# First norm factors loaded on GpSimd's queue, the LayerNorm's mean product half a block later, and the last norm's first third in a bank of its own

## The chip, the cores and the metric

One NeuronCore of a Trainium2 chip runs the whole program. The metric is the device time of one execution in microseconds (us), the median of three runs; lower is better.

## What is computed

One step of a hybrid decoder layer (depth 1) over 288 tokens: 256 new ones of a prompt and 8 x 4 of running samples. The model width is 2048, everything is fp32.

```python
h = rmsnorm(x, norm1_g)
a, gate, z = split(h @ w_in + b_in)                # 1024, 1024, 1024 columns
u = a * sigmoid(gate)
c = silu(layernorm(depthwise_causal_conv(u_ext, conv_w, conv_b), ln_g, ln_b))
d = multiscale_pool(z_ext)                         # windows 2, 4, 8, 16
p = (d @ pool_w per group) * pool_scale
x = x + concat[c, p] @ w_out
x = x + square(relu(rmsnorm(x, norm2_g) @ w_ff1)) @ w_ff2      # 8192 wide
y = rmsnorm(x, norm_f)
```

`rmsnorm` divides each token by the root of its mean square and multiplies by a gain per channel (the norm factors); `layernorm` needs the mean over 1024 channels first and then the mean of the squared differences. The last values of `u` and `z` go out as new states.

## The kernel before

**Layout.** Channels lie on the 128 partitions and the 288 tokens along the row, so x is the tile `xT` with 16 rows of 288 per partition. A product is one TensorE matmul of a 128x128 weight block with a 128x288 piece of activations.

**Two parts per number.** Every weight and every activation is split into `hi` (rounded to fp32r) and `lo` (the rest), and each pair of blocks takes three matmuls, hi.hi, lo.hi and hi.lo. A weight block of 512 KB comes in by DMA on SyncE's queue (`wr`), ScalarE rounds it to `whi` (L273), and VectorE or GpSimd subtracts to get `wlo` (L277, L281). There are five `whi` and five `wlo` buffers, so ScalarE's next rounding waits until TensorE has finished with the weights of five splits earlier. One such half block feeds 24 matmuls.

**Order.** The code runs through a scheduler that orders each engine's instructions by its own clock model; `tc.issue_after` puts an instruction behind a named other one, so a change at one place also moves rows elsewhere. `gemm` (L309) lists its matmuls; its `between={k: f}` calls `f` ahead of the matmuls of row block k, so that a small foreign product (a sum over channels) is put in there, and `classes` picks, place by place, the next matmul of a given parity of k and part (`TURN` is such a list, 48 long).

**The start.** SyncE's queue first loads the first norm's 16 columns of factors (`vec[:, 0:NG]`, 8 KB, L198), then in turns two rows of x (`xT`, L191) and two half blocks of weights (`wr`, L187); ScalarE's queue loads the first half block itself. Meanwhile 12 fp32 matmuls of ones keep TensorE busy (`warm`, L214; each shows as two records). `first_split` (L360) rounds the weights (ScalarE L365 and L372), makes the first activations `hx` from x and the factors (VectorE L368 for row 0, ScalarE L370 for the others), and subtracts for the low parts (VectorE L374, L377).

**The LayerNorm.** While TensorE multiplies the pooled half with `w_out` in eight blocks g = 0 to 7 (48 matmuls each), VectorE ends the convolution (L478), adds up `sum_c` over channel groups (L605), and a product with ones makes the mean over channels (tile `pmean`, in `ln_mean`, L601). It stands at the very front of block 4. `ln_sums` (L608) then subtracts the mean (VectorE L611), squares (ScalarE L613), adds the squares (VectorE L617, L618), splits the sum (L251, L252) and ends with two products (tile `norm`) at the front of block 6.

**The end.** After the last block the square sums of 288 tokens go through TensorE (L756), ScalarE and VectorE (L761 to L764) to 3 x 96 factors, which three small fp32 products spread over the partitions into `rows_f` (the tile `ends`, L767) and three more into `again`. VectorE multiplies rows 0 to 11 of `xT` by `rows_f` in pieces of 1, 1, 2, 2, 3 and 3 rows (L775); ScalarE copies `again` to `rf` for GpSimd, which takes rows 12 to 15. Each piece is written out at once, on SyncE's and ScalarE's queues in turns (L776). `idle` is a PSUM tile whose first 128 columns take three matmuls that only keep TensorE busy.

## Time and profile before

| what | value |
|---|---|
| median of 3 runs | 1078.71 us (1078.56 to 1078.87) |
| the profiled execution | 1078.44 us, of which the profile's span is 1076.7 |
| TensorE busy, matmul records | 1066.2 us (99%), 8176 |
| VectorE, ScalarE, GpSimd busy | 628.2, 482.2 and 180.0 us |
| first real matmul starts | 6.40 us into the span |
| last factors' spreading starts | 1066.00 us |
| mean granted TensorE clock | 0.997 |

Times in the profile count from the span's start. A row of the timeline has start, duration, engine and line, operation, the tiles written and read, the count of merged instructions, and in square brackets how long the engine had been idle and who ended that. PE is TensorE, DVE VectorE, ACT ScalarE, POOL GpSimd, SP SyncE; a q behind the name is the engine's queue or sequencer. Ends of matmuls are modelled, so starts are the better mark.

### The profile page before, as it was taken

How to read it: one execution, taken by the hardware profiler on the slowest of the kernel's cores; microseconds unless marked ns; L12 is line 12 of the kernel's file. 1: busy time of each engine (PE TensorE's matmuls, PEld its weight loads, DVE VectorE, ACT ScalarE, POOL GpSimd, SP SyncE). 2: the span in 40 equal slices, each digit the busy share in tenths (PEclk: the TensorE clock that was granted, in tenths of full speed). 3: DMA queues.
4: the chain of work that ended last, by engine and by line, in shares of the span. 5: the costliest groups of instructions: out<-in, count | busy, mean ns of one | idle time of the engine just before them, and what ended most of it. 6: DMA issues, size and time to landing. Idle time of an engine off the chain costs nothing.

```text
span 1076.7 us, 19546 instructions
## 1 busy us (share of the span) xinstructions
PE 1066.2 (99%) x8176; PEld 1065.5 (99%) x8176; DVE 628.2 (58%) x799; ACT 482.2 (45%) x598; POOL 180.0 (17%) x192
## 2 busy tenths in 40 slices
PE   9999999999999999999999999999999999999996
PEld 9999999999999999999999999999999999999996
DVE  8899998878554544445554444455444445554553
ACT  8655654755544433334443333444433334444441
POOL 0989889423000000000000000000000000000001
PEclk9999999999999999999999999999999999999998
DMA  9897777555455555555545555555555555455522
GB/s 333 292 248 217 223 183 244 178 174 170 164 174 165 171 172 164 174 164 169 175 165 170 170 166 175 167 166 176 162 172 171 165 174 169 164 176 162 172 80 89
DMA packets 58873, 192.81 MB, mean 179 GB/s; under 512 B 6304, under 2 KB 11296, under 8 KB 58784
## 3 DMA queue, kind: packets, MB, share of 16 engines
q1 hardware_dynamic: 56336, 184.35, 52.6%
q0 software_dynamic: 1584, 5.77, 2.9%
q8 instruction: 64, 1.05, 0.4%
q10 hardware_dynamic: 864, 1.44, 0.4%
q14 instruction: 25, 0.20, 0.1%
HBM read 187.25 MB, written 4.28 MB: 178 GB/s over the span
## 4 chain that ended last, share of the span: by engine, by line
PE 79%; issue 20%; POOL 0%; DVE 0%; POOLq 0%
PE ac L304 78%; PE pp L304 1%; PE warm L214 1%; POOL xT L775 0%; POOLq L825 0%; DVE xT L748 0%; PE norm L304 0%; PE pmean L304 0%; PE mean L304 0%; DVE ones L204 0%; DVE cst L232 0%; POOLq L775 0%; DVE cst L231 0%
## 5 line engine op out<-in xcount | busy, mean ns | idle before, releaser
L273 ACT CAST whi<-wr 128x1024 fp32r<-128x1024 f32 (+1 forms) x332 | 346.4, 1043 | 541.5 <-PE ac L304 524.6
L277 DVE TENSOR_TENSOR wlo<-wr,whi 128x1024 fp32r<-128x1024 f32 x282 | 346.2, 1228 | 349.3 <-ACT whi L273 349.2
L304 PE MATMUL ac<-ax,whi 128*128 128x288 f32 x2048 | 351.1, 292 | 0.0
L304 PE MATMUL ac<-fx,whi 128*128 128x288 f32 x2048 | 350.2, 292 | 0.0
L304 PEld LDWEIGHTS ac<-ax,whi 128*128 128x128 f32 x2048 | 296.0, 187 | 0.0
L304 PEld LDWEIGHTS ac<-fx,whi 128*128 128x128 f32 x2048 | 295.7, 187 | 0.0
L304 PE MATMUL ac<-ax,wlo 128*128 128x288 f32 x1024 | 217.4, 292 | 0.0
L304 PE MATMUL ac<-fx,wlo 128*128 128x288 f32 x1024 | 216.4, 292 | 0.0
L304 PEld LDWEIGHTS ac<-ax,wlo 128*128 128x128 f32 x1024 | 162.6, 187 | 0.0
L304 PEld LDWEIGHTS ac<-fx,wlo 128*128 128x128 f32 x1024 | 162.3, 187 | 0.0
L775 POOL TENSOR_TENSOR xT<-xT,rf 128x288 f32<-128x288 f32 x4 | 3.1, 791 | 786.6 <-ACT rf L779 786.6
L304 PE MATMUL ac<-hx,whi 128*128 128x288 f32 x768 | 130.1, 293 | 0.0
L304 PEld LDWEIGHTS ac<-hx,whi 128*128 128x128 f32 x768 | 110.6, 187 | 0.2
L281 POOL TENSOR_TENSOR wlo<-wr,whi 128x512 fp32r<-128x512 f32 x78 | 104.3, 1394 | 19.9 <-ACT whi L273 17.4
L478 DVE SCALAR_TENSOR_TENSOR pc<-u_all,vec,pc 128x256 f32<-128x256 f32 x232 | 99.3, 481 | 5.0 <-ACT pc L475 3.6
L304 PE MATMUL ac<-hx,wlo 128*128 128x288 f32 x384 | 79.5, 292 | 0.0
L304 PEld LDWEIGHTS ac<-hx,wlo 128*128 128x128 f32 x384 | 60.3, 187 | 0.1
L304 PE MATMUL ac<-dx,whi 128*128 128x288 f32 x256 | 45.9, 294 | 0.0
L304 PE MATMUL ac<-mx,whi 128*128 128x288 f32 x256 | 44.5, 292 | 0.0
L711 DVE SCALAR_TENSOR_TENSOR t<-ac,r 128x576 f32<-128x576 f32 x32 | 24.2, 757 | 25.4 <-PE ac L304 25.3
L304 PEld LDWEIGHTS ac<-dx,whi 128*128 128x128 f32 x256 | 38.1, 188 | 0.1
L304 PEld LDWEIGHTS ac<-mx,whi 128*128 128x128 f32 x256 | 37.4, 187 | 0.0
(142 smaller groups left out, 541.8 us busy)
## 6 DMA issues: line engine op xcount, KB each, us to landing
wr<-in_w SPq DMA_DIRECT2D x335, 512.0 KB, 3.6
wlo<-in_w POOLq DMA_DIRECT2D x11, 512.0 KB, 9.3
xT<-in_xT SPq DMA_DIRECT2D x8, 288.0 KB, 7.3
wr<-in_w SPq DMA_DIRECT2D x5, 256.0 KB, 4.0
out_u_out<-u_all SPq DMA_DIRECT2D x1, 1208.0 KB, 8.9
u_all<-in_hist_c SPq DMA_DIRECT2D x8, 136.0 KB, 5.5
out_z_out<-z_all SPq DMA_DIRECT2D x1, 668.0 KB, 8.6
z_all<-in_hist_p SPq DMA_DIRECT2D x4, 152.0 KB, 6.9
```

The lines of the kernel that those rows point to most:

```text
L214: nc.tensor.matmul(warm[:, 0, 0:P], ones, ones, start=True, stop=True)
L273: nc.scalar.copy(hi, raw)
L277: nc.vector.tensor_tensor(lo, raw, f32(hi), op=ALU.subtract)
L281: nc.gpsimd.tensor_tensor(lo[:, j : j + 2, :], raw[:, j : j + 2, :], f32(hi[:, j : j + 2, :]), op=ALU.subtract)
L304: last = nc.tensor.matmul(*args, **kw)
L478: nc.vector.scalar_tensor_tensor(out=dst, in0=up[:, w : w + SEQ], scalar=cwv[:, w : w + 1], in1=pc, op0=ALU.mult, op1=ALU.add)
L711: nc.vector.scalar_tensor_tensor(out=t, in0=bk[:, :, :T], scalar=0.0, in1=both(rows2[0]), op0=ALU.max, op1=ALU.mult)
L775: eng.tensor_tensor(xk, xk, r[:, None, :].to_broadcast([P, n, T]), op=ALU.mult)
```

## The change

Four edits. The load of the first norm factors moves from SyncE's queue to GpSimd's, so that x is the first load on SyncE's queue; in `first_split` the row-0 activations come ahead of the weight subtraction on VectorE, and the second rounding of a pair behind the ScalarE activations. `ln_mean` is called ahead of row block 4 of w_out block 4 instead of row block 0, and `TURN` goes from block 4 to block 5. At the end the first 96 of the 288 last factors are spread into a part of `idle` (`ahead_f`, another PSUM bank than `ends`); VectorE multiplies the first 96 tokens of rows 0 to 3 by them first, then tokens 96 to 287 of the pieces as before, with the first 96 tokens of rows 4 to 11 in between.

```diff
--- before.py
+++ after.py
@@ -195,7 +195,7 @@
             first_weights(k, nc.scalar, slice(0, 1))
             first_weights(k, nc.sync, slice(1, 2))
 
-    nc.sync.dma_start(vec[:, 0:NG], io["vec"][:, 0:NG])
+    nc.gpsimd.dma_start(vec[:, 0:NG], io["vec"][:, 0:NG])
     for k in range(0, 12, 2):
         first_load(k)
 
@@ -365,13 +365,15 @@
         nc.scalar.copy(hi[:, blocks[0]], raw[:, blocks[0]])
         for k in range(k0, k0 + 2):
             if k == 0:
-                nc.vector.tensor_scalar(hx[k][0], xT[:, k, :], v("norm1_g", k), None, op0=ALU.mult)
+                opening = [nc.vector.tensor_scalar(hx[k][0], xT[:, k, :], v("norm1_g", k), None, op0=ALU.mult)]
             else:
                 scaled.append(nc.scalar.activation(hx[k][0], xT[:, k, :], AF.Copy, scale=v("norm1_g", k)))
         for b in blocks[1:]:
-            nc.scalar.copy(hi[:, b], raw[:, b])
+            with tc.issue_after(scaled[-1].ins):
+                nc.scalar.copy(hi[:, b], raw[:, b])
         for b in blocks:
-            nc.vector.tensor_tensor(lo[:, b], raw[:, b], f32(hi[:, b]), op=ALU.subtract)
+            with tc.issue_after(opening[0].ins) if k0 == 0 else nullcontext():
+                nc.vector.tensor_tensor(lo[:, b], raw[:, b], f32(hi[:, b]), op=ALU.subtract)
         for k in (k0 + 1, k0):
             hh, hl = hx[k]
             nc.vector.scalar_tensor_tensor(out=hl, in0=xT[:, k, :], scalar=v("norm1_g", k), in1=f32(hh), op0=ALU.mult, op1=ALU.subtract)
@@ -619,13 +621,13 @@
         norm["rows"], last = row_of_sums(ssc[:, 0, :], "norm2", None, float(DC) / D, AF.Silu, parts=True)
         return last
 
-    BETWEEN = {4: {0: ln_mean}, 6: {0: ln_sums}}
+    BETWEEN = {4: {4: ln_mean}, 6: {0: ln_sums}}
     behind = nullcontext()
     for g in range(8):
         bk = bks[g] if g < 2 else bank2()
         if g > 1:
             with behind:
-                last = gemm(each(bk), proj, between=BETWEEN.get(g, {}), classes=TURN if g in (4, 6) else "")
+                last = gemm(each(bk), proj, between=BETWEEN.get(g, {}), classes=TURN if g in (5, 6) else "")
         behind = tc.issue_after(last) if g > 3 else nullcontext()
         x2 = xT[:, 2 * g : 2 * g + 2, :]
         nc.vector.tensor_tensor(x2, x2, bk[:, :, :T], op=ALU.add)
@@ -751,6 +753,7 @@
     ends, again = ms("ends"), cvp.tile([P, 512], F32, name="again", tag="cv")[:, :T]
     sums_f, rows_f = ends[:TB, 0, 0:3], ends[:, 1, :T]
     idle = cvp.tile([P, 512], F32, name="idle", tag="cv")
+    ahead_f = idle[:, P : P + TB]
     for n, (part, busy) in enumerate(((ssf, 0), (qf, 3))):
         for j in range(3):
             last = nc.tensor.matmul(sums_f[:, j : j + 1], part[:, j * TB : (j + 1) * TB], mean_d[:, 0:1], start=n + j == 0, stop=n == 1 and j == 2)
@@ -764,18 +767,28 @@
     nc.vector.scalar_tensor_tensor(out=s_f, in0=root, scalar=1.5, in1=first, op0=ALU.add, op1=ALU.mult)
     for spread_f in (rows_f, again):
         for j in range(3):
-            nc.tensor.matmul(spread_f[:, j * TB : (j + 1) * TB], s_f[:, j : j + 1].to_broadcast([TB, P]), ident, start=j == 0, stop=j == 2)
+            out = ahead_f if j == 0 and spread_f is rows_f else spread_f[:, j * TB : (j + 1) * TB]
+            nc.tensor.matmul(out, s_f[:, j : j + 1].to_broadcast([TB, P]), ident, start=j == 0 or out is not ahead_f and j == 1 and spread_f is rows_f, stop=j == 2 or out is ahead_f)
     rf = row("rf")
     queues = (nc.sync, nc.scalar)
 
-    def finish(eng, r, pieces):
-
-        for j, (k0, n) in enumerate(pieces):
-            xk = xT[:, k0 : k0 + n, :]
-            eng.tensor_tensor(xk, xk, r[:, None, :].to_broadcast([P, n, T]), op=ALU.mult)
-            queues[j % 2].dma_start(io["yT"][:, k0 : k0 + n, :], xk)
-
-    finish(nc.vector, rows_f, ((0, 1), (1, 1), (2, 2), (4, 2), (6, 3), (9, 3)))
+    def times(eng, r, k0, n, t0=0):
+
+        xk = xT[:, k0 : k0 + n, t0 : t0 + r.shape[1]]
+        return eng.tensor_tensor(xk, xk, r[:, None, :].to_broadcast([P, n, r.shape[1]]), op=ALU.mult)
+
+    def finish(eng, r, pieces, t0=0, j0=0):
+
+        for j, (k0, n) in enumerate(pieces, j0):
+            done = times(eng, r, k0, n, t0)
+            queues[j % 2].dma_start(io["yT"][:, k0 : k0 + n, :], xT[:, k0 : k0 + n, :])
+        return done.ins
+
+    times(nc.vector, ahead_f, 0, 4)
+    last = finish(nc.vector, rows_f[:, TB:], ((0, 1), (1, 1), (2, 2)), TB)
+    with tc.issue_after(last):
+        times(nc.vector, ahead_f, 4, 8)
+    finish(nc.vector, rows_f[:, TB:], ((4, 2), (6, 3), (9, 3)), TB, 1)
     nc.scalar.copy(rf, again)
     finish(nc.gpsimd, rf, [(k, 1) for k in range(12, KT)])
 
```

The line numbers of the changed code run on by 2 in the middle and by 3 and more at the end (L613 becomes L615, L775 becomes L778).

On VectorE's engine the first rows, before and then after: `wlo_170` and `whi_169` belong to the first weights, `hx_171` to rows 0 and 1 of x.

```order
L228 TENSOR_SCALAR means<-ones 128x128
L374 TENSOR_TENSOR wlo_170<-wr_93,whi_169 128x512
L368 TENSOR_SCALAR hx_171<-xT,vec 128x288
L377 SCALAR_TENSOR_TENSOR hx_171<-xT,vec,hx_171 128x288 x2
L374 TENSOR_TENSOR wlo_170<-wr_93,whi_169 128x512
```

```order
L228 TENSOR_SCALAR means<-ones 128x128
L368 TENSOR_SCALAR hx_171<-xT,vec 128x288
L379 SCALAR_TENSOR_TENSOR hx_171<-xT,vec,hx_171 128x288
L376 TENSOR_TENSOR wlo_170<-wr_93,whi_169 128x512
L379 SCALAR_TENSOR_TENSOR hx_171<-xT,vec,hx_171 128x288
L376 TENSOR_TENSOR wlo_170<-wr_93,whi_169 128x512
```

The activation that needs x and the factors (L368) now stands first, ahead of the subtraction of the first weights. On GpSimd the load (L198) becomes the first instruction after the program's branch, ahead of all its memsets.

On ScalarE's engine around the LayerNorm's squares, before and then after: `whi_2594` and `whi_2599` are the weights of w_out block 6, `whi_2658` and `whi_2663` those of block 7, `q_2671` to `q_2682` the squares of the four channel groups, `hl_2687` the high part of their sum.

```order
L273 CAST whi_2594<-wr_2590 128x1024
L613 ACTIVATE q_2671<-c_636 128x576
L613 ACTIVATE q_2674<-c_719 128x576
L613 ACTIVATE q_2678<-c_1018 128x576
L273 CAST whi_2599<-wr_2592 128x1024
L613 ACTIVATE q_2682<-c_1716 128x576
L273 CAST whi_2658<-wr_2654 128x1024
L251 CAST hl_2687<-q_2671 128x288
L273 CAST whi_2663<-wr_2656 128x1024
```

```order
L273 CAST whi_2594<-wr_2590 128x1024
L273 CAST whi_2599<-wr_2592 128x1024
L615 ACTIVATE q_2671<-c_636 128x576
L615 ACTIVATE q_2674<-c_719 128x576
L615 ACTIVATE q_2678<-c_1018 128x576
L273 CAST whi_2658<-wr_2654 128x1024
L615 ACTIVATE q_2682<-c_1716 128x576
L273 CAST whi_2663<-wr_2656 128x1024
L251 CAST hl_2687<-q_2671 128x288
```

Against the roundings of the weights each square stands one rounding later, and so does L251. On TensorE the two `norm` products keep their place at the front of block 6.

On VectorE's engine the last rows, before and then after: `ends_11504` is the tile of the spread factors, `idle` the other bank.

```order
L764 SCALAR_TENSOR_TENSOR cst<-cst 96x3
L775 TENSOR_TENSOR xT<-xT,ends_11504 128x288 x2
L775 TENSOR_TENSOR xT<-xT,ends_11504 128x576 x2
L775 TENSOR_TENSOR xT<-xT,ends_11504 128x864 x2
L825 UNCONDITIONAL_BRANCH
```

```order
L767 SCALAR_TENSOR_TENSOR cst<-cst 96x3
L778 TENSOR_TENSOR xT<-xT,idle 128x4x96
L778 TENSOR_TENSOR xT<-xT,ends_11504 128x192 x2
L778 TENSOR_TENSOR xT<-xT,ends_11504 128x2x192
L778 TENSOR_TENSOR xT<-xT,idle 128x8x96
L778 TENSOR_TENSOR xT<-xT,ends_11504 128x2x192
L778 TENSOR_TENSOR xT<-xT,ends_11504 128x3x192 x2
L838 UNCONDITIONAL_BRANCH
```

Six instructions become eight over the same 3456 elements per partition, and the first needs one spread product instead of three.

## The prediction

> **What bounds the kernel now.** I read the page first, then TensorE in two stretches, then the timelines of the start, of the LayerNorm and of the end.
>
> ```profile
> PE 1066.2 (99%) x8176; PEld 1065.5 (99%) x8176; DVE 628.2 (58%) x799; ACT 482.2 (45%) x598; POOL 180.0 (17%) x192
> ```
>
> TensorE is the only full engine. Since ends of matmuls are modelled, I count starts (the number in brackets), before and after the `pmean` product:
>
> ```profile
> 6.40:188.40 182.00, 182.00 (x1395) 1.00 0.84 251
> 188.40:1063.60 875.20, 875.20 (x6730) 1.00 0.50 164
> ```
>
> That is 182.00 / 1395 = 130.5 ns and 875.20 / 6730 = 130.0 ns from one matmul to the next, at full granted clock (1.00). From 6.40 to 1063.6 there is no hole. So the time is three parts: 6.4 us until the first real matmul, 1057.2 us of matmuls whose number doesn't change, and 13 us of tail. The edits can gain only in the first and the last, and lose in the middle, if something late makes TensorE wait. The one row where it hardly has any spare is `pmean`:
>
> ```profile
> 187.81 0.46 DVE L605 TENSOR_TENSOR sum_c<-pmean,c 128x288 f32<-128x288 f32 x1
> 188.60 0.75 DVE L631 TENSOR_TENSOR xT<-xT,ac 128x576 f32<-128x576 f32 x1 [0.34 <-PE ac L304]
> 189.27 2.74 DVE L611 TENSOR_TENSOR c<-c,pmean 128x576 f32<-128x576 f32 x4
> 191.93 3.91 DVE L617 TENSOR_TENSOR q<-q,q 128x576 f32<-128x576 f32 x3
> 195.88 1.43 DVE L618 TENSOR_TENSOR q<-q 128x288 f32<-128x288 f32 x1
> 197.23 0.74 DVE L631 TENSOR_TENSOR xT<-xT,ac 128x576 f32<-128x576 f32 x1
> 197.90 0.88 DVE L252 TENSOR_TENSOR hl<-q,hl 128x288 fp32r<-128x288 f32 x1
> ```
>
> ```profile
> 188.40 0.68 PE L304 MATMUL pmean<-sum_c,ones 128*128 128x288 f32 x2
> ...
> 201.49 0.42 PE L304 MATMUL norm<-hl,means 128*128 128x288 f32 x2
> ```
>
> Its input is done at 187.81 + 0.46 = 188.27, 0.13 us ahead of its start. The other end of that chain has room: L252 ends at 198.78, and `norm` starts at 201.49, 2.7 us later.
>
> **Edit 1, the start.** TensorE, SyncE's queue, ScalarE and VectorE:
>
> ```profile
> 1.06 5.43 PE L214 MATMUL warm<-ones 128*128 128x128 f32 x24 [1.06 <-DVE cst L232]
> 6.40 0.77 PE L304 MATMUL ac<-hx,whi 128*128 128x288 f32 x4
> ```
>
> ```profile
> 0.74 0.39 SPq L198 DMA_DIRECT2D vec<-in_vec  x1
> 1.18 0.42 SPq L191 DMA_DIRECT2D xT<-in_xT  x1
> ```
>
> ```profile
> 4.63 0.62 ACT L365 CAST whi<-wr 128x512 fp32r<-128x512 f32 x1 [1.95 <-DMA wr<-in_w]
> 5.45 0.54 ACT L370 ACTIVATE hx<-xT,vec 128x288 fp32r<-128x288 f32 x1 [0.20 <-DMA xT<-in_xT]
> 6.53 0.62 ACT L372 CAST whi<-wr 128x512 fp32r<-128x512 f32 x1 [0.55 <-DMA wr<-in_w]
> ```
>
> ```profile
> 1.04 1.51 DVE L228 TENSOR_SCALAR means<-ones 128x128 fp32r<-128x128 f32 x1
> 5.28 0.69 DVE L374 TENSOR_TENSOR wlo<-wr,whi 128x512 fp32r<-128x512 f32 x1 [2.73 <-ACT whi L365]
> 5.89 0.36 DVE L368 TENSOR_SCALAR hx<-xT,vec 128x288 fp32r<-128x288 f32 x1
> ```
>
> All loads on SyncE's queue move up by 1.18 - 0.74 = 0.44 us, so x lands at about 5.0 instead of 5.45, and L368, now ahead of L374, may start there instead of at 5.89. By that alone the first matmul could come 0.9 us earlier. It can't: the 24 warm-up records run from 1.06 with modelled ends to 6.49, and the first real matmul already starts inside that. One record is 5.43 / 24 = 0.23 us of pace, so TensorE's queue is free no earlier than 6.2. The gain is at most 0.2 us, and I take 0.1. The earlier second half block (L372) only keeps the matmuls behind it fed.
>
> The price lies with the factors. L370 and L368 wait for them, and behind these two stand in order L372 and all later ScalarE and VectorE work of the start. They land now, and GpSimd's other loads (512 KB each) land, after their issue:
>
> ```profile
> vec<-in_vec SPq DMA_DIRECT2D x1, 8.0 KB, 3.5
> ```
>
> ```profile
> DMA to landing us min/median/max: 6.5/9.3/11.0
> ```
>
> The second row is that of the 11 loads of L275. So the landing is bounded by 0.74 + 3.5 = 4.2 us (a gain is excluded, since TensorE is busy until 6.2) and 0.74 + 11.0 = 11.7. The transfer is 64 times smaller than GpSimd's, so I stay by the first row, with an estimated 1 us more for GpSimd's part: 5.2. Anything up to 5.9, where L368 starts now, costs nothing; later costs its lateness, 7.2 (the least) 1.35 us and 10.0 (the median) 4.15 us. On GpSimd's queue the load delays only memsets that nobody needs in this stretch. One thing beside it could hold it: L228, 1.51 us long for 128 columns next to GpSimd's memsets. If the load can be written out only when L228 has ended, it lands 1.51 us later, at 6.7, and the first matmul loses 0.8 us.
>
> The Trainium skill's page "SBUF — State Buffer", section "SBUF: two separate sides", speaks against this edit: while VectorE runs an operation that uses both ports on one operand, GpSimd can't write the descriptors of its loads, which the hardware queues don't suffer. By that rule the wait for L228 would be real and the term +0.8 instead of -0.1; no row here shows a GpSimd load beside such an operation.
>
> **Edit 2, the mean half a block later.** 24 matmuls of 0.130 us are 3.1 us: `pmean` goes to 188.40 + 3.12 = 191.52, and `norm` stays. TensorE loses nothing by the order itself (all turned stretches together cost the 0.5 ns between the two paces above). L605 now has 3 us to spare, so small moves of VectorE's convolution rows before it, and one 1.05 us rounding that slips ahead of L238, cost nothing. What is late next is the rest of the chain, whose room was 2.7 us. ScalarE's rows:
>
> ```profile
> 192.34 1.05 ACT L273 CAST whi<-wr 128x1024 fp32r<-128x1024 f32 x1 [0.21 <-PE ac L304]
> 193.29 0.69 ACT L613 ACTIVATE q<-c 128x576 f32<-128x576 f32 x1
> 195.49 1.05 ACT L273 CAST whi<-wr 128x1024 fp32r<-128x1024 f32 x1 [1.52 <-issue]
> 197.34 0.43 ACT L251 CAST hl<-q 128x288 fp32r<-128x288 f32 x1 [0.80 <-DVE q L618]
> 198.62 1.06 ACT L273 CAST whi<-wr 128x1024 fp32r<-128x1024 f32 x1 [0.84 <-PE ac L304]
> ```
>
> The roundings are paced by TensorE (one per 3.12 us, as buffers come free), and the fourth square now stands behind the one at 195.49. So it starts at about 196.45 and ends at 197.13, not at 193.98: 3.15 us later. From the fourth square's end to L252's end it took 198.78 - 193.98 = 4.80 us. Added to 197.13 that is 201.93. L252's result feeds the second `norm` product, due 0.13 after the first, at 201.62. TensorE waits 201.93 - 201.62 = 0.3, with 0.1 for the signal 0.4 us. The bounds come from this row of L617:
>
> ```profile
> L617 DVE TENSOR_TENSOR q<-q,q x3: 757/1282/1664, 191.9 to 194.2; 128x576 f32<-128x576 f32 x3
> ```
>
> The three equal additions take 0.76 to 1.66 us. If the last takes 0.76, as do L618 and L252 in that proportion, the chain ends by about 200.6 and there is no wait; if all take the longest, with the addition of block 4's result (L631, 0.74, now between the first and second L617), it ends at about 202.6: a wait of 1.0.
>
> The page "GPSIMD Engine Reference" of the Trainium skill, section "Specifications", says that VectorE's operations with two SBUF inputs contend with GpSimd for its interface. L617 agrees (1.66 us against 0.76, GpSimd subtracting alongside); as GpSimd has as many subtractions 3 us later, by that rule the 4.80 us would be repeated, and the sum with it.
>
> **Edit 3, the end.**
>
> ```profile
> 1066.00 0.91 PE L767 MATMUL ends<-ident,cst 96*128 96x96 f32 x6 [0.22 <-DVE cst L764]
> ```
>
> ```profile
> 1066.94 4.08 DVE L775 TENSOR_TENSOR xT<-xT,ends 128x288 f32<-128x288 f32 x6 [1.00 <-PE ends L767]
> ```
>
> ```profile
> L775 DVE TENSOR_TENSOR xT<-xT,ends 128x864 f32<-128x864 f32 x2 | 2.0, 1044 | 0.0
> L775 DVE TENSOR_TENSOR xT<-xT,ends 128x576 f32<-128x576 f32 x2 | 1.4, 746 | 0.0
> ```
>
> ```profile
> 1068.25:1069.00 0.75, 0.00 (x0) 0.00 (x0) 0.75 (x2) 0.00 (x0) 0.75 (x2) 1.00 0.98 349
> 1069.00:1069.25 0.25, 0.00 (x0) 0.00 (x0) 0.25 (x2) 0.00 (x0) 0.25 (x1) 1.00 0.41 134
> 1069.25:1074.25 5.00, 0.00 (x0) 0.00 (x0) 1.77 (x2) 0.00 (x0) 1.90 (x3) 0.70 1.03 395
> ```
>
> VectorE now waits for six spread records; waiting for two saves four of 0.13, so it starts 0.5 us earlier, at 1066.44. A piece costs 1.03 ns per element (1044 - 746 over 288) and about 0.07 us more; eight pieces instead of six take 4.24 instead of 4.08 us. The last then ends at 1070.7 instead of 1071.0, the first output piece 0.13 and the third 0.43 us earlier; the fourth, behind the eight rows of 96, comes 0.24 us later. But from 1069.25 on the outputs bound the end: the last three rows show 395 GB/s with all 16 DMA engines full. What was lost before is (395 - 349) x 0.75 + (395 - 134) x 0.25 = 100 KB, or 0.25 us. That hole and the 0.13 us are all that can be gained, 0.4 us; the later fourth piece can open the hole again. I take -0.25, between +0.1 (the fourth piece's delay at some 40% of the rate) and -0.5 (the last GpSimd piece no longer queues behind the last VectorE piece on ScalarE's queue).
>
> **Sum.** -0.1 + 0.4 - 0.25 = +0.05 us on the profiled execution's 1078.44, so 1078.49. The median lies 0.27 above that execution: 1078.76, rounded 1078.8. A measurement of this kernel tells some 0.2% (2.2 us) from no change.
>
> **Rivals.**
> - The LayerNorm chain keeps up (the short L617): -0.1 - 0.25, so 1078.4. For it: L251 alone could start at 199.6, right behind the last rounding ahead of it. Against: the 4.80 us that the same rows took. 0.23.
> - The chain is late by its bound of 1.0: 1078.71 + 1.0 - 0.1 - 0.25, so 1079.4. 0.10.
> - Slower: the factors land late on GpSimd's queue, and TensorE's first matmul with them. From a landing at 5.9 it costs, from 8.1 on (7.3 us after issue) more than 0.2%; at GpSimd's median, 1078.71 + 4.15, it gives 1082.9. For it stand the 11 loads, none under 6.5 us; against it their size. 0.08, half of it past 8.1.
> - The factors wait for L228 as priced above: 1078.71 + 0.8 + 0.4 - 0.25, so 1079.7. This is what the page on SBUF gives. 0.05.
> - The warm-up is no floor and TensorE starts with x, 0.44 us earlier: 1078.71 - 0.44 - 0.25 gives 1078.0 if the chain keeps up too. Against: the start inside the warm-up's modelled end. 0.03.
>
> **How the numbers follow.** The forecast has 0.51. The range reaches from 1078.0 (front -0.2, tail -0.5, no wait), less 0.15 for the spread of the runs, to the factors landing at 7.2 (1078.71 + 1.35, rounded up): 1077.9 to 1080.2. Past 0.2% slower only the late factors lead, 0.04, with 0.01 for what no row shows on either side: slower 0.05, faster 0.01, within 0.2% 0.94.
>
> **What would show it.** In the changed profile the first real matmul should start between 6.2 and 6.4, L368 before 5.9; `norm` should start with its second product some 0.4 us late and nowhere else a hole between 6.4 and 1063; VectorE's first piece 0.4 us after the spreading starts, and the DMA rate near 395 GB/s without the dip at 1069. I am wrong if L368 starts after 6, if `pmean` or any other product waits, or if the time is over 2.2 us away.

## The result, and the profile after

The changed kernel takes 1081.52 us (median of 11 runs, 1080.43 to 1083.30), the kernel before 1078.71 beside it (11 runs, 1078.44 to 1079.49). The ratio, taken over all runs, is 1.0023 with a 95% interval from 1.0015 to 1.0031: slower by some 2.5 us (2.8 between the medians). The profiled execution took 1081.44, with a span of 1079.6 (before: 1078.44 and 1076.7).

TensorE's work is the same, 8176 records:

```profile
PE 1066.8 (99%) x8176; PEld 1065.4 (99%) x8176; DVE 629.2 (58%) x801; ACT 482.1 (45%) x598; POOL 181.5 (17%) x193
```

So what was added lies between its records. Counted from the first real matmul at 130.0 ns for each, the two traces part as follows (us):

| stretch | before | after | added |
|---|---|---|---|
| first real matmul | 6.40 | 7.21 | 0.81 |
| lost from there to about 112 | 0.69 | 0.75 | 0.06 |
| lost from 112 to 165 | 0.00 | 0.74 | 0.74 |
| lost from 165 to 219 | 0.54 | 2.43 | 1.89 |
| lost from 219 to the spreading | 0.19 | 0.18 | -0.01 |
| spreading to the end of the span | 10.67 | 10.14 | -0.53 |
| sum | | | 2.96 |

**The start.** The timelines of TensorE, GpSimd, ScalarE and VectorE, and the load's row (the last figure is the time from issue to landing):

```profile
1.06 4.47 PE L214 MATMUL warm<-ones 128*128 128x128 f32 x24 [1.06 <-DVE cst L232]
7.21 0.51 PE L304 MATMUL ac<-hx,whi 128*128 128x288 f32 x2 [1.68 <-DVE hx L368]
```

```profile
1.26 0.75 POOL L198 DMA_DIRECT2D vec<-in_vec  x1 [0.81 <-POOLq L834]
```

```profile
5.60 0.62 ACT L365 CAST whi<-wr 128x512 fp32r<-128x512 f32 x1 [2.92 <-DMA wr<-in_w]
6.70 0.53 ACT L370 ACTIVATE hx<-xT,vec 128x288 fp32r<-128x288 f32 x1 [0.48 <-DMA vec<-in_vec]
```

```profile
6.70 0.37 DVE L368 TENSOR_SCALAR hx<-xT,vec 128x288 fp32r<-128x288 f32 x1 [5.43 <-DMA vec<-in_vec]
```

```profile
vec<-in_vec POOLq DMA_DIRECT2D x1, 8.0 KB, 5.4
```

L368 waits for `vec`, no longer for x: the factors land at 1.26 + 5.4 = 6.7. The first weights are late too (L365 at 5.60 instead of 4.63). The warm-up ends at 5.5, and TensorE then stands still for 1.7 us.

**A slip and a slower pace.** At 139.78 one of TensorE's starts comes 0.11 us late, between the two `wlo` matmuls of the second row here, which wait for a low part that GpSimd adds by DMA (L275):

```profile
139.13 0.55 PE L304 MATMUL ac<-hx,whi 128*128 128x288 f32 x3
139.54 0.54 PE L304 MATMUL ac<-hx,wlo 128*128 128x288 f32 x2
```

Behind it the starts are no longer 130.0 ns apart, but 133.3, until the `TURN` products at 168. The windows of TensorE show it as five matmuls fewer in the same 24 us (before first, then after; the clock is at 1.00 in both):

```profile
141.00:165.00 24.00, 24.00 (x187) 1.00 0.73 203
```

```profile
141.00:165.00 24.00, 24.00 (x182) 1.00 0.71 185
```

**The LayerNorm.** `pmean` comes at 193.23 and waits for nothing. Then VectorE, ScalarE and TensorE:

```profile
193.91 2.75 DVE L613 TENSOR_TENSOR c<-c,pmean 128x576 f32<-128x576 f32 x4 [2.48 <-PE pmean L304]
196.58 1.26 DVE L619 TENSOR_TENSOR q<-q,q 128x576 f32<-128x576 f32 x1
197.76 0.74 DVE L633 TENSOR_TENSOR xT<-xT,ac 128x576 f32<-128x576 f32 x1
198.43 3.62 DVE L619 TENSOR_TENSOR q<-q,q 128x576 f32<-128x576 f32 x2
202.09 1.43 DVE L620 TENSOR_TENSOR q<-q 128x288 f32<-128x288 f32 x1
204.02 0.95 DVE L252 TENSOR_TENSOR hl<-q,hl 128x288 fp32r<-128x288 f32 x1 [0.50 <-ACT hl L251]
```

```profile
197.23 1.05 ACT L273 CAST whi<-wr 128x1024 fp32r<-128x1024 f32 x1 [0.46 <-POOL wlo L281]
198.19 0.68 ACT L615 ACTIVATE q<-c 128x576 f32<-128x576 f32 x1
```

```profile
198.36 6.29 POOL L281 TENSOR_TENSOR wlo<-wr,whi 128x512 fp32r<-128x512 f32 x4 [1.14 <-ACT whi L273]
```

```profile
203.11 0.29 PE L304 MATMUL ac<-dx,whi 128*128 128x288 f32 x1
204.04 0.40 PE L304 MATMUL norm<-hl,means 128*128 128x288 f32 x1 [0.64 <-ACT hl L251]
205.02 0.40 PE L304 MATMUL norm<-hl,means 128*128 128x288 f32 x1 [0.59 <-DVE hl L252]
```

The two `norm` products start 0.93 and 0.98 after the matmul ahead of each instead of 0.13: together 1.66 us of waiting. While VectorE makes the second and third addition (L619, 3.62 us for the two), GpSimd subtracts beside them.

**The end.** VectorE's pieces start 0.50 behind the spreading (1069.50), where it was 0.94:

```profile
1070.00 0.55 DVE L778 TENSOR_TENSOR xT<-xT,idle 128x384 f32<-128x384 f32 x1 [0.55 <-PE idle L771]
1070.47 1.07 DVE L778 TENSOR_TENSOR xT<-xT,ends 128x192 f32<-128x192 f32 x3
1071.47 0.94 DVE L778 TENSOR_TENSOR xT<-xT,idle 128x768 f32<-128x768 f32 x1
1072.33 1.87 DVE L778 TENSOR_TENSOR xT<-xT,ends 128x384 f32<-128x384 f32 x3
```

### The profile page after: what moved, and what is told of

It is laid out like the page before. It is cut to its first block, busy times and chain, and to the rows that moved or that the text cites. A ratio compares the mean times of both kernels' runs of the same rounds, so it can differ in the third digit from the quotient of the medians.

```text
span 1079.6 us, 19547 instructions
## 1 busy us (share of the span) xinstructions
PE 1066.8 (99%) x8176; PEld 1065.4 (99%) x8176; DVE 629.2 (58%) x801; ACT 482.1 (45%) x598; POOL 181.5 (17%) x193
## 4 chain that ended last, share of the span: by engine, by line
PE 77%; issue 20%; DVE 1%; DMA 1%; POOL 0%; POOLq 0%; ACT 0%; DVEq 0%
PE ac L304 77%; PE pp L304 1%; DMA vec<-in_vec 1%; DVE q L619 0%; DVE c L613 0%; POOL xT L778 0%; DVE q L620 0%; DVE hl L252 0%; PE norm L304 0%; POOLq L838 0%; DVE xT L750 0%; PE pmean L304 0%; ACT hl L251 0%; DVE hx L368 0%; PE mean L304 0%
## 5 line engine op out<-in xcount | busy, mean ns | idle before, releaser
L778 POOL TENSOR_TENSOR xT<-xT,rf 128x288 f32<-128x288 f32 x4 | 3.0, 796 | 786.6 <-DVE xT L778 786.6
```

What stands on the lines that cost most here:

```text
L778: return eng.tensor_tensor(xk, xk, r[:, None, :].to_broadcast([P, n, r.shape[1]]), op=ALU.mult)
```

## The experiments

Times are medians (of 6 runs in e13 and e17, of 11 in the others), with those of the kernel before on the same chip beside them. The ratio is over all runs, not the quotient of the medians. What the text says of waits and paces comes from one profiled execution of each. e15 and e16 are single executions and stand below. Line numbers in the rows are those of each kernel.

| run | us | before | ratio, 95% interval |
|---|---|---|---|
| e1 | 1080.63 | 1079.45 | 1.0011 [1.0002, 1.0020] |
| e2 | 1081.07 | 1079.45 | 1.0010 [1.0001, 1.0019] |
| e3 | 1078.85 | 1079.45 | 0.9998 [0.9990, 1.0007] |
| e4 | 1081.29 | 1079.45 | 1.0017 [1.0008, 1.0026] |
| e5 | 1079.63 | 1078.87 | 1.0001 [0.9993, 1.0010] |
| e6 | 1081.31 | 1078.87 | 1.0018 [1.0008, 1.0027] |
| e7 | 1081.69 | 1078.87 | 1.0025 [1.0016, 1.0034] |
| e8 | 1081.74 | 1078.87 | 1.0020 [1.0011, 1.0029] |
| e9 | 1081.44 | 1079.17 | 1.0018 [1.0009, 1.0027] |
| e10 | 1079.61 | 1079.17 | 1.0001 [0.9992, 1.0010] |
| e11 | 1079.70 | 1079.17 | 1.0007 [0.9998, 1.0016] |
| e12 | 1078.71 | 1079.17 | 0.9997 [0.9989, 1.0006] |
| e13 | 1082.64 | 1079.29 | 1.0032 [1.0020, 1.0043] |
| e14 | 1079.88 | 1079.29 | 1.0010 [1.0001, 1.0019] |
| e17 | 1081.95 | 1078.71 | 1.0031 [1.0019, 1.0043] |
| e18 | 1080.88 | 1078.71 | 1.0020 [1.0011, 1.0028] |

### The start: e4, e1, e6, e7, e14

e4, the kernel before with one line changed:

```diff
-    nc.sync.dma_start(vec[:, 0:NG], io["vec"][:, 0:NG])
+    nc.gpsimd.dma_start(vec[:, 0:NG], io["vec"][:, 0:NG])
```

> The kernel before with the factors' load on GpSimd's queue alone, without the turned order in first_split. Theory: the load's packets start only about 1 us after GpSimd's memsets have ended, so the factors land at 6.5 to 6.8 and the first real matmul starts at 7.2 to 7.5 instead of 6.40: 0.8 to 1.1 us more, 1079.5 to 1079.8, if no wait elsewhere opens. Rival: the turned order is what delayed the start; then the factors land by 5.9 and the time is 1078.7.

The factors landed at 6.7, the first real matmul started at 7.23: the line alone makes the 0.8 of the start. The rest of its time is the slip at 139.84 and a wait that belongs to the LayerNorm, below.

e1, the changed kernel with that line turned back:

> The changed kernel with one line undone: the factors load from SyncE's queue again, first there; the turned order on VectorE and ScalarE, the later mean and the new tail stay. Theory: the late landing of the factors (6.67) is the whole loss at the start, so L368 starts below 5.9, the first real matmul at 6.2 to 6.4 instead of 7.21, and about 0.8 us of the 3 go. If the hole at 139.78 and the slow stretch behind it (133.3 ns a matmul to 165.5) came from the shifted start as well, they go too: 1.7 us in all, 1079.8. Rival: the loss is that of the new order in first_split; then the first matmul stays at 7.2 and the time at 1081.5.

The first real matmul started at 6.20, and the slip at 139.8 and its slow stretch were gone. The time is only 0.9 below the changed kernel's, since two other things stood in its trace: the first matmuls, up to 7.05, still ran at half clock (starts 240 ns apart), and there was a slip of 0.3 at 76.5 with a slow stretch to 84. The `norm` products waited as in the changed kernel.

e6 puts one instruction between the load and GpSimd's memsets; e7 also moves L228 to ScalarE:

```diff
+    touch = const.tile([P, 1], F32, name="touch")
+    landed = nc.gpsimd.tensor_copy(touch, vec[:, 0:1]).ins
...
-    nc.vector.tensor_scalar(means, ones, -0.5 * DC / D, None, op0=ALU.mult)
+    nc.scalar.activation(means, ones, AF.Copy, scale=-0.5 * DC / D)
```

> The changed kernel, with a one-column copy of the factors as GpSimd's first instruction behind the load, so that GpSimd waits for the landing and its memsets come after it. Theory: the packets of a GpSimd load start only when the instructions queued right behind it are done; with nothing running behind it they start about 0.2 us after the load's own 0.76 us, at about 2.2 instead of 4.78, the factors land at about 4.1 instead of 6.67, L368 starts with x at 5.4 and the first real matmul at 6.0 to 6.4: 0.8 to 1.2 us less than 1081.5. Rival: 3.5 us to the first packet is what a GpSimd load takes; then the landing stays at 6.7 and the time at 1081.5.

> As the run with the quiet GpSimd, and the scaling of the ones (L228) on ScalarE instead of VectorE, so that nothing of two ports runs on VectorE beside the load. Theory: the load's start at 1.26 was L228's end (1.27); without it the load starts at 0.75 to 1.05, and the factors land that much earlier, 3.6 to 3.9. Rival: the 0.5 us between the branch and the load is GpSimd's own; then it starts at 1.26 again. The time shows no difference between the two, since x is the later one.

Both theories fell. With GpSimd idle behind the load (first row, e6: it waits 4.57 us for the landing) the factors landed as late as before, and without L228 (second row, e7) the load started no earlier:

```profile
6.57 0.18 POOL L216 COPY touch<-vec 128x1 f32<-128x1 f32 x1 [4.57 <-DMA vec<-in_vec]
```

```profile
1.25 0.75 POOL L198 DMA_DIRECT2D vec<-in_vec  x1 [0.81 <-POOLq L837]
```

e14 is the kernel before with the new tail and

```diff
-    nc.sync.dma_start(vec[:, 0:NG], io["vec"][:, 0:NG])
     for k in range(0, 12, 2):
         first_load(k)
+        if k == 0:
+            nc.scalar.dma_start(vec[:, 0:NG], io["vec"][:, 0:NG])
```

together with e5's pin, below.

> The kernel before with the new tail, the factors' load on ScalarE's queue behind the first half block, and the mean's input held ahead of block 3's addition. Theory: the factors land before x (by 5.4), so the first real matmul starts at 6.2 to 6.9; the tail is shorter by 0.4 because SyncE's queue has one load fewer, not because of GpSimd: 10.1 to 10.2 from the spreading to the end of the span instead of 10.55. With the row order alone as cause, the slip at 139.8 appears here too (+0.8); then 1079.0 in all, without it 1078.2. Rival for the tail: GpSimd's load is what matters; then 10.55 again.

The first part of the theory fell. The same load on ScalarE's queue took as long as on GpSimd's, and the first real matmul started at 7.53 (e14 first, then e1, where it is the first load on SyncE's queue):

```profile
vec<-in_vec ACTq DMA_DIRECT2D x1, 8.0 KB, 5.4
```

```profile
vec<-in_vec SPq DMA_DIRECT2D x1, 8.0 KB, 3.8
```

So a late landing doesn't need GpSimd's queue. In the changed kernel and in e14 x and the first weights are issued ahead, from 0.74; in the changed kernel the 16 DMA engines are busy at 0.88 and more from 2.5 us on. The factors' first packets appear at 4.8 there, and at 4.6 in e14, where the load also stands behind the first half block of weights on its own queue. Issued first, on SyncE's queue, they took 3.1 to 4.1 us in seven traces and passed x.

That the place in line makes the difference fits all of this, but it is argued. No run issues this load first on GpSimd's queue, so e6's rival, a long way to the first packet on GpSimd's queue whatever else is loading, isn't excluded: five loads of L275 in the changed kernel that found no other on their queue showed their first packets 2.3 to 3.9 us after issue, where the factors took 3.5.

Behind the factors x loses nothing: it lands between 5.33 and 5.80 in the traces with the load on GpSimd's queue, and between 5.36 and 5.90 with the load ahead of it on SyncE's (e9 left out, whose other load holds it up). So the factors ahead of x cost x nothing, and behind x they come 1.3 us after it in the changed kernel.

### The mean and the norm products: e2, e5, e10, e11

e2, the changed kernel with `BETWEEN = {4: {0: ln_mean}, ...` and `TURN` in block 4 again:

> The changed kernel with the mean product back at the front of block 4 and TURN back in block 4; load, start and tail as changed. Theory: the two waits of the norm products (0.80 and 0.86) go, and the pace of blocks 4 and 5 returns from about 132.6 to 130.0 ns: 1.8 us less, 1079.7, with the first matmul at 7.2 and the slow stretch from 139.8 still there. Rival: the chain was late because the whole kernel before it had shifted; then the norm products still wait over 1 us and the time is within 0.3 of the changed kernel's.

Neither. The `norm` products waited no more, but `pmean` now did, 1.4 us, and the profiled execution took 1081.28 against 1081.44. VectorE's and TensorE's rows say for whom:

```profile
189.14 0.48 DVE L480 SCALAR_TENSOR_TENSOR c<-u_all,vec,pc 128x256 f32<-128x256 f32 x1
190.51 0.76 DVE L633 TENSOR_TENSOR xT<-xT,ac 128x576 f32<-128x576 f32 x1 [0.89 <-PE ac L304]
191.18 0.45 DVE L607 TENSOR_TENSOR sum_c<-pmean,c 128x288 f32<-128x288 f32 x1
```

```profile
191.69 0.51 PE L304 MATMUL pmean<-sum_c,ones 128*128 128x288 f32 x1 [1.21 <-DVE sum_c L607]
```

The convolution was done at 189.62, but the scheduler now has block 3's addition (L633) ahead of the mean's input (L607), and that addition waits for TensorE to end the block. In the kernel before L605 stands first, in e4 as here second:

```
before: L605 sum_c<-pmean_2538,c_1716   L631 xT<-xT,ac_2473
e4:     L631 xT<-xT,ac_2473             L605 sum_c<-pmean_2538,c_1716
```

e5 is e2 with the old order pinned: the input part of `ln_mean` becomes a function of its own, `ln_parts`, and is called ahead of the addition of g = 3:

```diff
+        with tc.issue_after(ln_parts().ins) if g == 3 else nullcontext():
-        nc.vector.tensor_tensor(x2, x2, bk[:, :, :T], op=ALU.add)
+            nc.vector.tensor_tensor(x2, x2, bk[:, :, :T], op=ALU.add)
```

> The run with the mean product back at the front of block 4, and on VectorE the mean's input (L605 of the kernel before) held ahead of block 3's addition to xT, as it stands in the kernel before; load, start and tail as changed. Theory: the 1.50 us for which pmean waited in the two runs with the mean at the front and the load on GpSimd's queue came from that addition, which the scheduler had put ahead and which itself waits for TensorE to end block 3; pinned, pmean waits under 0.2, the norm products wait under 0.2, and the time is 1.5 below those runs: 1079.6. Rival: VectorE's convolution as a whole is late by as much; then pmean still waits over 1 us and the time stays at 1081.1.

Right to 0.03 us: 1079.63, and neither `pmean` nor `norm` waits. The slow pace behind 139.8 stayed, behind a slip of only 0.04 us: two starts at 139.64 and 139.81, 0.17 apart instead of 0.13.

```profile
189.53 0.46 DVE L607 TENSOR_TENSOR sum_c<-pmean,c 128x288 f32<-128x288 f32 x1
190.32 0.75 DVE L636 TENSOR_TENSOR xT<-xT,ac 128x576 f32<-128x576 f32 x1 [0.33 <-PE ac L304]
```

e10 leaves GpSimd's subtractions out (zeros for the low parts of three blocks' weights), e11 holds the roundings behind the fourth square (for that it lists the squares and additions already at row block 6 of block 5; only the lines on the roundings are shown):

```diff
+                if way == "Z":
+                    nc.gpsimd.memset(f32(lo[:, j : j + 2, :]), 0.0)
...
+        with tc.issue_after(squared[-1].ins) if squared else nullcontext():
-        nc.scalar.copy(hi, raw)
+            nc.scalar.copy(hi, raw)
```

> The changed kernel, with GpSimd writing zeros into the low parts of the weights of w_out blocks 5, 6 and 7 (pooled half) instead of subtracting; those low parts are left out of the result. Theory: the additions of the LayerNorm chain are long (1.26, 1.84, 1.67 and 1.43 us, L252 0.95) because GpSimd subtracts beside them; without that they take 0.76, 0.76, 0.76 and 0.4, the chain ends about 2 us earlier, and the norm products wait under 0.3 instead of 1.66: 1.4 to 1.7 us less, 1080.0. Rival: the chain hangs on the fourth square, half a block late; then the additions may be short, but the second norm product still waits 0.8 or more.

> The changed kernel with the fourth square (L615 of the changed kernel) held ahead of the rounding of block 7's weights on ScalarE, so that it starts right behind the third one, 1.0 to 1.5 us earlier. The prediction's step: that square is what the chain waits for, so the norm products wait 1.0 less or not at all: 0.8 to 1.6 us less, about 1080.3. Theory now: VectorE's additions are last, each queued behind the one before; the third starts when the second ends, so the norm products wait 1.66 as before, and the time stays at 1081.5.

e10 came out by its theory. Its fourth square starts at 198.22, as late as in the changed kernel (198.19), and yet no `norm` product waits: with short additions a square that late costs nothing. The groups of VectorE from 193 to 206 (mean ns of one behind the comma), after and e10:

```profile
L619 DVE TENSOR_TENSOR q<-q,q 128x576 f32<-128x576 f32 x3 | 4.8, 1593 | 0.1
L620 DVE TENSOR_TENSOR q<-q 128x288 f32<-128x288 f32 x1 | 1.4, 1431 | 0.0
L252 DVE TENSOR_TENSOR hl<-q,hl 128x288 fp32r<-128x288 f32 x1 | 1.0, 952 | 0.5 <-ACT hl L251 0.5
```

```profile
L623 DVE TENSOR_TENSOR q<-q,q 128x576 f32<-128x576 f32 x3 | 2.3, 754 | 0.2 <-ACT q L619 0.2
L624 DVE TENSOR_TENSOR q<-q 128x288 f32<-128x288 f32 x1 | 0.5, 459 | 0.0
L252 DVE TENSOR_TENSOR hl<-q,hl 128x288 fp32r<-128x288 f32 x1 | 0.5, 457 | 1.5 <-ACT hl L251 1.5
```

Beside GpSimd's subtractions the same additions take 1593 instead of 754 ns, 1431 instead of 459. This is the contention of which the page "GPSIMD Engine Reference" of the Trainium skill speaks in "Specifications", and here are its sizes, two to three times the duration without the subtractions. VectorE's own subtractions of the mean (L613), which read one input from PSUM, keep 0.75 us each in the changed kernel, with GpSimd subtracting beside them as well.

In e11 the theory "now" fell, and the prediction's step was right: with the square ahead nothing waits, and the time is 1.8 lower. But it is not the square's own earliness alone. The rounding that stood ahead of it at 197.23 is what GpSimd's subtraction waits for (198.36); held back, it lets the second and third addition run before GpSimd's next subtraction, which starts at 199.46 (e11):

```profile
198.31 1.61 DVE L620 TENSOR_TENSOR q<-q,q 128x576 f32<-128x576 f32 x2
199.95 1.44 DVE L621 TENSOR_TENSOR q<-q 128x288 f32<-128x288 f32 x1
201.89 0.96 DVE L252 TENSOR_TENSOR hl<-q,hl 128x288 fp32r<-128x288 f32 x1 [0.50 <-ACT hl L251]
```

1.61 us for the two instead of 3.62. One rounding put ahead of one square did both.

### The slip and the pace behind it: e9, e8, e13, e17, e18, e15, e16

e9, a late start with the order of before:

```diff
+    nc.scalar.dma_start(z_all[:].rearrange("p k t -> p (k t)")[:, 0:768].rearrange("p (k c) -> p k c", c=256), io["w"][6][:, 0:3, :])
```

> The kernel before with one more load, 384 KB of weights that nobody reads into a part of z_all, put first on ScalarE's queue: it takes about 1 us of the DMA engines and so delays x and the first weights, while the order of the instructions stays that of before on VectorE, GpSimd, ScalarE and TensorE but for the first few rows. Theory: the slip at 139.8 and the slow stretch behind it, and the late mean, come from the other order into which the scheduler puts VectorE's rows when the factors load on GpSimd's queue; with before's order a late start costs only itself: first matmul at 7.0 to 7.5, pace 130.0 ns from 140 to 165, no wait at pmean over 0.2, time 0.6 to 1.1 over before. Rival: a start later by 0.8 opens the slip by itself; then the pace from 140 to 165 is 133.3 and the time 1.5 to 2 over before.

In its profile the first matmul started at 7.92, with 130.0 ns from 140 to 165 and 0.14 at `pmean`; the execution took 1080.09, which is 1.65 over the kernel before's, of which the start is 1.52. So a late start alone need not open the slip. That execution is the fastest of its eleven, though (1080.09 to 1083.82), and what the others lost was not seen: the median is 2.3 over the kernel before beside it, more than the rival's 1.5 to 2.

e8 and e13 were meant for the slip and missed it: they change the products of pooling group 1, which end at 134.6, while those around 139.8 are group 0's.

```diff
-        gemm(each(bk), hx)
+        gemm(each(bk), hx, classes="." * 36 + TURN if g == 1 else "")
```

```diff
-"p0": "GDVG", "p"
+"p0": "GDVG", "p1": "GV", "p"
```

> The changed kernel with TURN put into the products of pooling group 1, 36 matmuls in, right behind the hole at 139.78. Theory: the hole only put TensorE into a slower alternation (133.3 instead of 130.0 ns a matmul), which the turned order takes it out of; behind it, from about 147 to 165.5, the pace is 130.0 again, and about 0.5 us go: 1081.0. Rival: the 133.3 ns come from work on other engines in that stretch; then the pace stays at 133 and the time at 1081.5.

> The changed kernel with VectorE instead of a GpSimd DMA making the low part of pooling group 1's second weight block (way V for D). Theory: the slip at 139.78 is the landing of that DMA, and the 133.3 ns behind it follow from the slip; without the DMA there is no slip there, the pace from 141 to 165 is 130.0, and 0.8 us go: 1080.7. VectorE has 1.2 us more work, which the later mean has room for. Rival: the slow pace comes from the row order (other engines' reads and writes), slip or no slip; then it stays at 133.3, and the time at 1081.5.

They still tell something, since the slip was there in both and larger. The transfer of L275 took, from issue to landing, in the changed kernel, e8 and e13:

```profile
DMA to landing us min/median/max: 7.6/7.6/7.6
```

```profile
DMA to landing us min/median/max: 8.1/8.1/8.1
```

```profile
DMA to landing us min/median/max: 9.3/9.3/9.3
```

It landed at 139.50, 140.15 and 140.78 and TensorE went on at 139.54, 140.20 and 140.82 (in the kernel before it took 6.5 and landed at 137.68, in time).

Over all traces the duration of this transfer goes with the queue of the first load. It is 5.9 to 6.5 us in the seven with the factors first on SyncE's queue (the kernel before, e1, e3, e9, e12, e15, e16) and 7.4 to 9.3 in the other twelve that have it. e14 is one of the twelve, though it loads the factors on ScalarE's queue, and e9 one of the seven, though it starts latest (first e14, then e9):

```profile
DMA to landing us min/median/max: 7.4/7.4/7.4
```

```profile
DMA to landing us min/median/max: 6.1/6.1/6.1
```

So it is neither GpSimd's load as such nor the late start that makes it long, and with e1 (6.2) not the turned order of the start either; why it is long without the factors on SyncE's queue is not known. All twelve traces with the load on GpSimd's queue have a slip between 134.8 and 141.6, none of the other eight. e14 has none, since its products come 0.3 us later (first real matmul at 7.53 instead of 7.21), enough for a landing at 139.55.

e17 and e18 put the same two edits into group 0, `"p0": "GVVG"` and `if g == 0`:

> The changed kernel with VectorE instead of a GpSimd DMA making the low part of pooling group 0's second weight block, the one that TensorE waited for at 139.8. Theory: no slip there, pace 130.0 from 141 to 165, 0.8 us less: 1080.7, with both norm waits still there. Rival: the slow pace belongs to the row order; then 133.3 again without a slip.

> The changed kernel with TURN in the products of pooling group 0, 36 matmuls in, so from about 140.9, behind the slip. Theory: the turned order ends the slow pace; from about 147 to 165 it is 130.0 instead of 133.3 ns, about 0.45 us less: 1081.0. Rival: the slow pace ends by something else around 168 (the change of operands from hx to dx); then 133.3 until then and 1081.5.

e18 came out by its theory: a slip of 0.42 at 139.8, the turned order behind it, and from 148 on 130.0 ns. In 16 us from 148 to 164 it has as many matmuls as the kernel before, the changed kernel four fewer (after, then e18):

```profile
148.00:164.00 16.00, 16.00 (x122) 1.00 0.83 200
```

```profile
148.00:164.00 16.00, 16.00 (x126) 1.00 0.85 185
```

e17 gained nothing. The slip at 139.8 was gone, but a smaller one, 0.08 us at 134.81, came ahead of it (the second matmul of the tile `pp`), and behind that the pace was 133.3 as well. A slip of 0.08 us is enough, and in e5 one of 0.04 was.

e15 and e16 are two looks at the kernel before itself, unchanged:

> The kernel before, unchanged, for a look at one more execution. If it takes 1078.4 to 1079.0, its trace is that already shown. If it takes 1080 or more, the theory is that TensorE's clock was granted late or taken back in the first 12 us (matmuls 0.24 apart instead of 0.13); the rival is a slip in the stage from 60 to 170 with the slow pace behind it.

> The kernel before, unchanged, a second look, as the one before this: at 1078.4 to 1079.0 the known trace; at 1080 or more a late clock in the first 12 us by the theory, a slip between 60 and 170 by the rival.

They took 1081.03 and 1078.52. The theory fell for the first: its clock was full from 5.4. The rival was right in kind, a slip with the slow pace behind it, but the slip came earlier than in the stage that it named. The same program in the same order, and one transfer of L275 that took 11.2 instead of 9.5 us made TensorE wait:

```profile
52.87 0.54 PE L304 MATMUL ac<-hx,wlo 128*128 128x288 f32 x2 [0.71 <-DMA wlo<-in_w]
```

From there to the next `TURN` (80 to 90) the pace is 133.3 (e15 first, then e16); from 92 to 118 both have 202 matmuls again:

```profile
54.00:80.00 26.00, 26.00 (x197) 1.00 0.89 241
```

```profile
54.00:80.00 26.00, 26.00 (x203) 1.00 0.94 255
```

So one program has both paces, the slow one follows a slip and not the row order, and the next `TURN` ends it, here as in e18. The turned order isn't a sure remedy, though: e15 also ran at 133.3 from 18.6 to 32, right behind the first turned stretch, with a slip of 0.11 at 10.18 ahead of that stretch.

### The tail: e3, and the rest: e12

e3 is the kernel before with the new tail alone:

> The kernel before with the changed tail alone. Theory: 0.55 us less (the changed kernel's trace showed the tail 0.59 shorter), 1078.15, with VectorE's first piece 0.5 after the spreading starts. Rival: the tail is bound by its transfers and gives the 0.25 of the forecast, or nothing: 1078.45 to 1078.7.

Its median is 0.6 below the kernel before's, but the ratio's interval holds no change. From the spreading to the end of the span says more, since it varies little between executions (us; the span's end less the first spreading record's start):

| | load on SyncE, first | on GpSimd | on ScalarE |
|---|---|---|---|
| old tail | 10.67, 10.63 (e9), 10.68 (e15), 10.68 (e16) | 10.31 (e4) | |
| new tail | 10.54 (e1), 10.56 (e3), 10.56 (e12) | 10.14, 10.15 (e2), 10.15 (e5), 10.19 (e6), 10.18 (e7), 9.99 (e10), 10.15 (e11), 10.13 (e18) | 10.24 (e14) |

Three more with the new tail and the load on GpSimd lie above: 10.35 (e8) and 10.81 (e17), where some of the last TensorE records are 0.2 us apart instead of 0.1, and 10.68 (e13). The new tail is worth 0.1 to 0.2 us. Another 0.3 to 0.4 go with the first factors' load not being on SyncE's queue, with old tail and new: the last two outputs, on ScalarE's queue, land 0.2 to 0.5 earlier then. e14's theory for the tail, one load fewer on SyncE's queue, is borne out by its 10.24, but why a load at the start should matter at the end is not known.

e12 is the changed kernel without its two losses (load as in e1, mean as in e5):

> The changed kernel with the factors' load first on SyncE's queue again and the mean product at the front of block 4 with its input held ahead of block 3's addition: what is left of the change is the turned order of the start and the new tail. Theory: none of the three losses is left (first matmul 6.2 to 6.9, pace 130.0 behind 140, no norm wait), and the tail gives 0.1 to 0.5, so 1078.2 to 1078.7, at or below the kernel before. Rival: the turned order of the start costs something of its own (a slip at 76.5 was seen with it); then 1078.9 to 1079.5.

1078.71, of which neither the theory nor the rival can be told: the ratio's interval holds no change. No norm wait and no slip at 139.8 were in its trace, but one of 0.73 at 8.47, where TensorE waited for the second half of the first weights (ScalarE's L373, which waited for their landing). It is no proven gain over the kernel before, and no version here is.

## Why the prediction was wrong

**Edit 1, -0.1 forecast, +0.81 measured: wrong.** The step that failed is "I stay by the first row, with an estimated 1 us more for GpSimd's part: 5.2". The factors landed at 6.7. That row (3.5 us) was of a load that stood first in line, before the DMA engines had anything to do; I carried its duration to a load that stands behind x and asked only what another queue would add. Of the 2.4 us between 4.2 and 6.7, 0.5 is the later issue (1.26 instead of 0.74) and 1.9 the longer transfer, 5.4 instead of 3.5. Behind x and the first weights ScalarE's queue takes 5.4 as well (e14); how much of the 1.9 is the place in line and how much GpSimd's own is open. The rival "the factors wait for L228" gave the right landing, 6.7, and the right 0.8 by a wrong mechanism: e7 has no L228 on VectorE and the load starts at 1.25 all the same. The rule of the Trainium skill's "SBUF — State Buffer" ("SBUF: two separate sides") that stood behind that rival is not what acted here. The late-factors rival had the right wait, a landing past 5.9, at a chance of 0.08; it was priced by GpSimd's large loads (6.5 us and more), where this one took 5.4.

The other half of the step failed as well. "TensorE's queue is free no earlier than 6.2" took the warm-up as fixed. In the changed kernel's trace it ended at 5.5, because the full clock came at 4.3 us (its starts go from 213 to 112 ns apart there); in the others it ended between 5.6 and 6.6. So the floor is not firm, though nothing here got below it: x lands no earlier.

**Edit 2, +0.4 forecast, 1.66 measured: right mechanism, one term mis-sized.** The fourth square was to end 197.13 - 191.52 = 5.61 behind `pmean`; it ended 198.87 - 193.23 = 5.64 behind it. From its end to L252's end I repeated 4.80; it took 204.97 - 198.87 = 6.10. The missing 1.3 us is the whole miss, and it made the first `norm` product wait too (0.80 for L251), which the sum didn't have. "The 4.80 us would be repeated" failed because the rounding ahead of the square moved GpSimd's subtractions onto the second and third addition (e10, e11); the bound of 1.0, the longest rows added up, was too small as well, since they became longer than any row before (3.62 for two). The mean at the front would not have been free either: beside the new load the scheduler's order would have made `pmean` wait 1.4 (e2). The rows of the changed kernel already have that order; I priced the later mean against the old one.

**"Nowhere else a hole between 6.4 and 1063": wrong, 0.74.** I read the 0.5 ns between the two paces as the cost of the turned stretches. They hide two paces, 130.0 and 133.3 ns, of which the kernel before's trace showed only the first. A slip of 0.11 us (0.04 in e5) started the second, and it lasted to the next turned stretch. What a late transfer costs here is some 25 us at 3.3 ns of 133.3, 0.6, and not its 0.1. The slip is another price of edit 1, which the prediction did not ask for: the transfer of L275 took 7.6 instead of 6.5, and it is longer in every trace without the factors on SyncE's queue. Why is open.

**Edit 3, -0.25 forecast: right in kind, smaller in size**, 0.1 to 0.2 by the table. The other 0.4 in the changed kernel's tail goes with the first edit, and was unforeseen; that the whole tail gained 0.5, the forecast's best case, is luck.

Put together: the sum of +0.05 missed 0.9 at the start, 0.1 behind it, 0.7 in the pace and 1.5 at the norm (1.3 of it the waits, the rest the slower pace of blocks 4 and 5), and got 0.3 back at the end: 2.9, by which the 2.96 of the table exceed it.

## What to carry to other kernels

A transfer's duration in a trace holds for its queue and its place in line: before a small load is moved behind a large one, look at what the DMA engines do between its issue and its landing. When an edit puts one rounding ahead of another step, ask which third engine that rounding sets free, and beside whose operations it will then run. And where a kernel has an order written out by hand in some stretches, find out what it repairs before calling its cost small; a slip of a tenth of a microsecond can cost several times itself.

## What was not expected of the hardware

- The same fp32r matmuls, 128x288 back to back at full granted clock, run at 130.0 or at 133.3 ns apart. Every slip seen outside the stretches ordered by hand, from 0.04 us (e5) on, was followed by the second pace. The next 48 matmuls in the turned order ended it; only e15's stretch from 18.6 to 32 began right behind such an order.
- TensorE's full clock came after 3.2 (changed kernel) to 6 us (e1) of warm-up, and can be lost again. In e7, after 1.84 us of standing still, the matmuls from 7.8 to 11.2 were 240 ns apart, at a granted clock of 0.56 over the window below, 1.5 us lost; after 1.68 in the changed kernel it stayed at 1.00 (e7, then after). Where the limit lies is not known.

```profile
7.40:11.20 3.80, 3.78 (x17) 0.56 1.05 407
```

```profile
7.20:11.00 3.80, 3.79 (x28) 1.00 1.05 406
```

- Which queue took the program's first 8 KB goes with the duration of a transfer at 131 us (1 us and more) and with the end of the program a thousand microseconds later (0.3 to 0.4 us).
